# Branch A's attention output loaded and split inside branch B's chunks of a hybrid encoder layer, other slots for branch B's, branch weights by the sync queue

## The chip, the cores and the metric

The kernel runs on one core of a Trainium2 chip. The metric is the device time of one execution in microseconds; lower is better. The engines are named as in the profile: PE (TensorE matmul) with PEld (its weight loads), DVE (VectorE), ACT (ScalarE), POOL (GpSimd) and SP (SyncE, which here only issues DMAs). "us" is microseconds.

## The reference

One layer over 1024 tokens of width 1024, in fp32:

```
h = x + 1/2 * SwiGLU_1(RMSNorm(x))                       # d_ff 2816
u = RMSNorm(h)
[qA|kA|vA|qB|kB|vB|gA|gB] = u @ W_in                      # A: 8 heads; B: 8 heads, 2 kv heads; gates 1024 each
yA = NeighbourhoodAttention2D(qA, kA, vA) + relative bias
yB = WindowedGQA(rope(qB), rope(kB), vB), sink in the softmax
h = h + (sigmoid(gA) * (yA @ W_A) + sigmoid(gB) * (yB @ W_B)) @ W_out
h = h + 1/2 * SwiGLU_2(RMSNorm(h))
y = RMSNorm_final(h)
```

yA and yB are 512 wide, W_A and W_B are 512 x 1024, W_out is 1024 x 1024.

## The kernel before, in words

Every operand of a matmul is split into a high part (a cast to fp32r on ACT, line 95) and a low part (the rest, a subtraction on DVE, line 98). `split` does this. `mm3` (lines 146 to 153) then issues three matmuls for each product: high by high on line 149, high by low on 151, low by high on 153. Activations stand transposed, features on partitions.

The program's order in time: first FFN, the input projection, the attention, the branch matrices, the merge with W_out, the second FFN, the last norm. This case is about the stretch from the end of the attention to the start of the merge.

Storage is in fixed places. `ar[0]` to `ar[6]` are seven large tiles of four slots each; slot k is a 128x1024 piece of `ar[k // 4]`. During the attention `ar[0]`, `ar[6]`, `ar[1]` and `ar[4]` hold u, split. Three pools have few buffers: `raw` (4, for tiles just loaded), `xs` (2) and `ws` (8, split weights and the attention's transposed probabilities). A load can be issued only once its buffer is free.

The attention (lines 1434 to 1461) is a pipeline of 64 units, each with the steps `scores` (matmuls on lines 1377 and 1378, softmax on DVE and ACT), `turn` (transposes on line 1396, then a split) and `values` (matmuls on line 1410, whose `write` puts the result into `fa` or a DRAM tensor `y_d`). Between a unit's steps `filling` draws from the generator `fill`, which issues other matmuls so that PE has work:

- `gate(dc, steps)`: 8 steps of 6 matmuls, one 128-wide piece of the gate projection from u; `steps` says what is issued behind which step. Steps 0 to 3 read `ar[1]` and `ar[4]` (c = 4 to 7), steps 4 to 7 read `ar[0]` and `ar[6]`. The result is copied to an `xs` tile (line 1207) and stored to `g_d`.
- `branch_b`: eight chunks of 24 matmuls, yB @ W_B. Chunk dc needs its split weights (`fetch_w(dc)`, a load of a 128x1024 tile of `wab_d`, split during the first FFN), and yB, split, in the four pairs of slots `Y_B`. Each chunk ends with two operations on DVE that multiply by the gate (line 1280) into `merged(dc)`; the gate's tile is loaded by `fetch_gate` and opened by a tanh on ACT (`open_gate`).
- three quarters of the first two chunks of branch A.

`fetch_y` loads a 128x1024 tile of an attention output from `y_d` into a `raw` buffer, `split_y` splits it into a pair of slots. Branch B's slots are 4 to 7 (`ar[1]`) and 0 to 3 (`ar[0]`). Branch A's first three pairs are split at units 59, 60 and 62 of the attention; the fourth is written by the last attention units themselves.

Behind the attention the loop on line 1495 runs the chunks of branch A (i = 0 to 7), adds them into `merged` and forms combinations (`combine`). Then `down` (class `Down`, 28 entries of 12 matmuls) multiplies by W_out with Strassen's seven products. Each entry e needs two splits, its `prep`.

The order of instructions on each engine comes from the tile framework, which schedules by its own estimates; `pin` (lines 92 and 97) holds an instruction in program order on its engine. Each engine, and each of the two DMA-issuing queues (SP and POOL), works through its list in that order and waits where something isn't ready.

Of the kernel before, what the change touches and what calls it, by code (L numbers as in the profile page):

```python
# [36 lines left out]
def trunk_kernel(ctx, tc, x, xt, n1, wg1, wu1, wd1, nm, win, rpb, sink, wa, wb, wo,  # L37
# [39 lines left out]
    def slot(k):  # L77
        return ar[k // 4][:, k % 4, :]
# [15 lines left out]
    def split(dst_hi, dst_lo, src, eng=None, late=False):  # L94
        hi = nc.scalar.copy(dst_hi, src)  # L95
        if late:
            pin(hi)
        (eng or nc.vector).tensor_tensor(dst_lo, src, f32v(dst_hi), op=ALU.subtract)  # L98
# [415 lines left out]
    class Down:  # L514
# [2 lines left out]

        ORDER = ("P2", "P1", "P5", "P6", "P3", "P7", "P4")

        def __init__(self, n, w, scale, place, left=None, dram=None, loads={}, ring=(22, 24, 26), shift=0):  # L520
# [5 lines left out]
            self.TAIL = min(n, 5)  # L526
            self.ring, self.shift, self.RING = ring, shift, 4 + len(ring)
            self.W = self.Y = None

# [31 lines left out]
        def prep(self, e):  # L561
            k, p = self.seq[e]
            if k in self.dram:
                d = self.dk.index(k) * self.nd + p // 2
                self.load_left(d + 3)
                left = self.raw[d][:, p % 2, :]
            else:
                left = self.left(k, p)
            b11, b12, b21, b22 = [self.blocks(n, p)[:, 0, :] if n in self.loaded else None for n in ("B11", "B12", "B21", "B22")]
            eng = nc.gpsimd if self.n > self.RING else nc.vector  # L570
            if k == "P5":
                nc.vector.tensor_tensor(b11, b12, b11, op=ALU.subtract)
# [7 lines left out]
            split(s[:, :512], s[:, 512:], left)  # L580
            split(t[:, :512], t[:, 512:], dict(B11=b11, B12=b12, B21=b21, B22=b22)[SOURCE[k]])
            self.ent[e] = s, t

        def prep_until(self, n):
# [134 lines left out]
    wab_d = dram.tile([2 * NC8, P, 1024], F32R, name="wab_d")  # L719
    cast = {}  # L720

    def hs(dt):
# [11 lines left out]

    def wab_put(i):
        for k, a in enumerate(cast.pop(i)):
            nc.gpsimd.dma_start(wab_d[i, :, k * 512:k * 512 + 512], a)

    def behind_ffn1(n):
        down.at_end(n)  # L740
# [466 lines left out]
            nc.scalar.copy(gt[:, n * 512:(n + 1) * 512], bs[n])  # L1207
        nc.gpsimd.dma_start(g_d[dc * P:(dc + 1) * P, :], gt)

    Y_A, Y_B = ((12, 13), (14, 15), (20, 21), (22, 23)), ((4, 5), (6, 7), (0, 1), (2, 3))  # L1210

    def branch_mm(bs, w, y):

# [23 lines left out]
        a_mm.append((bs, branch_mm(bs, mix.pop(("w", NC8 + i)), Y_A)))  # L1237

    def merged(dc):
        return slot((16, 17, 18, 19, 24, 25, 26, 27)[dc])  # L1240

    def fetch_gate(dc):
        mix["rb", dc] = xs4() if dc % 2 else raw4()
        nc.sync.dma_start(mix["rb", dc], g_d[D + dc * P:D + (dc + 1) * P, :])

    def fetch_w(i):
        t = ws4()
        nc.gpsimd.dma_start(t, wab_d[i])
        mix["w", i] = [t[:, k:k + 512].rearrange("p (c f) -> p c f", f=P) for k in (0, 512)]

    def open_gate(dc):
# [2 lines left out]

    def branch_b():

        for g in (4, 6):
            new_ar(g, F32)
        split_y(Y_B[2], 2 * P, nc.vector)
        fetch_w(1)  # L1260
        for dc in range(NC8):
            bs = [bank("dg"[dc % 2]) for _ in range(2)]
            mm = branch_mm(bs, mix.pop(("w", dc)), Y_B)
            for c in range(4):
                drain(mm, 1)
                yield
                if c == 0:
                    if dc == 0:
                        split_y(Y_B[3], 3 * P, nc.vector)
                        open_gate(0)  # L1270
                    if dc + 1 < NC8:
                        fetch_gate(dc + 1)
                elif c == 1:
                    fetch_w(dc + 2)
                elif c == 3 and dc + 1 < NC8:
                    open_gate(dc + 1)
            rb = mix.pop(("rb", dc))
# [13 lines left out]
    def filler():  # L1291
        for dc, nxt in zip(gates, gates[1:] + [None]):
            if nxt is not None:
                yield from gate(dc, {4: lambda: mix.update(gate=load_w(win[0], GA + nxt * P))})
            else:
                yield from gate(dc, {0: lambda: [fetch_y(c * P) for c in range(2)],
                                     1: lambda: [fetch_w(0), fetch_gate(0)],
                                     4: lambda: [split_y(Y_B[0], 0, nc.vector), fetch_y(2 * P)],
                                     6: lambda: [split_y(Y_B[1], P, nc.vector), fetch_y(3 * P)]})
        yield from branch_b()  # L1300
        for i in range(2):
            branch_a(i)
# [131 lines left out]
    for n in range(1 << 30):  # L1434
# [13 lines left out]
            drain(prep, 1)  # L1448
        if n >= 26 and (n - 26) % 8 == 0 and n < 58:
            fetch_bias((n - 26) // 8)  # L1450
        if n in (56, 57, 59):
            fetch_y(512 + min(n - 56, 2) * P)
        if n in (59, 60, 62):
            split_y(Y_A[min(n - 59, 2)], 512 + min(n - 59, 2) * P, nc.vector)
        filling(n)
        if len(pipe) > 2 and pipe[2] is not None:
            values(pipe[2])
# [17 lines left out]
    def quarter(k, p):  # L1475
        m = merged(p + (4 if k in ("P2", "P4") else 0))
        return m[:, :512] if k in ("P1", "P2") else m[:, 512:]

    place = dict(B11=[(0, p) for p in range(4)], B21=[(0, 4 + p) for p in range(4)],
                 B12=[(1, p) for p in range(4)], B22=[(1, 4 + p) for p in range(4)])  # L1480
    loads = {t: [lambda d, t=t: load_h(t)] for t in range(NTT)}
    loads[0].append(lambda d: d.load_left(2))
    down = Down(4, wo[0], 0.5, place, quarter, {k: left_d[i] for i, k in enumerate(("P5", "P6", "P3", "P7"))},
                loads, (8, 10))

    def combine(p):
        a11, a12, a22 = [quarter(k, p) for k in ("P1", "P2", "P4")]
# [163 lines left out]
```

## Time and profile before

| | |
|---|---|
| time, median of 3 runs | 1932.38 us (1932.32 to 1932.75) |
| the profiled execution's own time | 1933.77 us |
| its span in the profile | 1932.0 us |
| PE busy | 1919.7 us (99%) |
| DVE busy | 1435.3 us (74%) |
| ACT busy | 940.3 us (49%) |
| POOL busy | 301.4 us (16%) |
| mean granted PE clock | 0.998 |

The profile's times run from the start of the span. A row of the timeline gives start, duration, engine, line, operation, output and input tile, and in brackets how long the engine had been idle and what ended that. A row that ends in "x2" joins two instructions; the duration of such a row, and of single matmuls, runs longer than the distance to the next row, since matmuls are pipelined. So the price of a matmul is the distance between starts.

### The profile page before, as it was taken

What the parts mean: (1) busy time and instruction counts of PE and PEld (TensorE: products, weight loads), DVE (VectorE), ACT (ScalarE), POOL (GpSimd) and SP (SyncE); (2) the same over time, 40 slices, a digit from 0 to 9 for tenths busy, and PEclk for the clock granted to TensorE, in tenths of its full rate; (3) what the DMA queues carried; (4) which work ended last, traced back from release to release, by engine and by line L of the source; (5) the groups of instructions that cost most, each with busy time, mean ns of one, the idle gap of its engine ahead of it and who ended that gap; (6) DMA issues with size and microseconds to landing.
All of it is one profiled execution on the core that took longest, in us unless ns stands there. A gap on an engine that the chain in (4) does not pass through costs nothing.

```text
span 1932.0 us, 25630 instructions
## 1 busy us (share of the span) xinstructions
PE 1919.7 (99%) x8956; PEld 1603.0 (83%) x8956; DVE 1435.3 (74%) x2511; ACT 940.3 (49%) x1826; POOL 301.4 (16%) x466
## 2 busy tenths in 40 slices
PE   9999999999999999999999999999999999999998
PEld 7888888888888888888888878888888888888886
DVE  8987766668966878677788846989676566569864
ACT  7532444444446543477788842365333333344453
POOL 0011111214400112211122011010111001005210
PEclk9999999999999999999999999999999999999999
DMA  6254556586454267854478386543422322492341
GB/s 267 94 173 166 176 177 193 172 294 246 124 171 150 108 200 239 257 163 99 115 174 202 135 297 234 180 153 120 147 96 102 130 86 106 143 354 103 114 143 61
DMA packets 163330, 321.78 MB, mean 167 GB/s; under 512 B 16256, under 2 KB 69888, under 8 KB 163200
## 3 DMA queue, kind: packets, MB, share of 16 engines
q1 hardware_dynamic: 127744, 216.82, 34.3%
q0 software_dynamic: 34736, 102.26, 16.4%
q8 instruction: 71, 1.16, 0.2%
q10 hardware_dynamic: 720, 1.05, 0.1%
q14 instruction: 59, 0.48, 0.1%
HBM read 222.04 MB, written 99.81 MB: 167 GB/s over the span
## 4 chain that ended last, share of the span: by engine, by line
PE 96%; DVE 2%; DMA 1%; ACT 1%; issue 0%; POOLq 0%; SPq 0%; POOL 0%; DVEq 0%
PE g L149 18%; PE g L151 18%; PE g L153 18%; PE d L153 12%; PE d L151 12%; PE d L149 12%; PE d L1396 2%; PE g L1415 1%; PE d L1377 1%; PE d L1378 1%; PE g L1410 1%; PE d L142 1%; DVE ar L98 0%; DMA raw<-y_d 0%; DMA raw<-in_w_in_dram 0%
## 5 line engine op out<-in xcount | busy, mean ns | idle before, releaser
L149 PE MATMUL g<-ar,ws 128*128 128x512 f32 x1128 | 423.2, 395 | 0.1
L153 PE MATMUL g<-ar,ws 128*128 128x512 f32 x1128 | 417.6, 390 | 0.0
L151 PE MATMUL g<-ar,ws 128*128 128x512 f32 x1128 | 417.6, 390 | 0.0
L149 PE MATMUL d<-ar,ws 128*128 128x512 f32 x736 | 282.3, 391 | 1.5 <-ACT ar L95 1.4
L151 PE MATMUL d<-ar,ws 128*128 128x512 f32 x736 | 282.0, 390 | 0.9 <-DVE ar L879 0.6
L153 PE MATMUL d<-ar,ws 128*128 128x512 f32 x736 | 281.8, 390 | 0.1
L153 PEld LDWEIGHTS g<-ar,ws 128*128 128x128 f32 x1128 | 212.0, 188 | 45.2
L151 PEld LDWEIGHTS g<-ar,ws 128*128 128x128 f32 x1128 | 212.0, 188 | 44.5
L149 PEld LDWEIGHTS g<-ar,ws 128*128 128x128 f32 x1128 | 206.6, 188 | 36.5 <-ACT xs L1207 0.6
L322 DVE TENSOR_TENSOR ws<-raw,ws 128x512 fp32r<-128x512 f32 x204 | 139.4, 689 | 83.4 <-ACT ws L319 82.5
L319 ACT CAST ws<-raw 128x512 fp32r<-128x512 f32 x204 | 125.2, 620 | 142.8 <-PE g L153 63.0
L149 PEld LDWEIGHTS d<-ar,ws 128*128 128x128 f32 x736 | 138.0, 188 | 31.0 <-ACT ar L95 1.8
L151 PEld LDWEIGHTS d<-ar,ws 128*128 128x128 f32 x736 | 138.1, 188 | 30.6 <-DVE ar L879 1.3
L153 PEld LDWEIGHTS d<-ar,ws 128*128 128x128 f32 x736 | 138.4, 188 | 29.7 <-DVE ws L322 0.8
L95 ACT CAST ws<-raw 128x512 fp32r<-128x512 f32 (+1 forms) x111 | 74.7, 673 | 137.0 <-PE d L153 62.9
L98 DVE TENSOR_TENSOR ws<-raw,ws 128x512 fp32r<-128x512 f32 (+1 forms) x111 | 89.1, 803 | 53.7 <-ACT ws L95 52.9
L426 POOL DMA_DIRECT2D hid<-fx x91 | 49.4, 543 | 373.1 <-DVE fx L486 247.4
L98 DVE TENSOR_TENSOR ws<-ar,ws 128x512 fp32r<-128x512 f32 x114 | 93.8, 828 | 11.5 <-ACT ws L95 11.5
L95 ACT CAST ar<-raw 128x512 fp32r<-128x512 f32 (+1 forms) x81 | 54.1, 670 | 88.5 <-PE g L151 54.4
L149 PE MATMUL g<-ws,ws 128*128 128x512 f32 x232 | 90.9, 392 | 0.0
L153 PE MATMUL g<-ws,ws 128*128 128x512 f32 x232 | 90.4, 390 | 0.0
L151 PE MATMUL g<-ws,ws 128*128 128x512 f32 x232 | 90.3, 389 | 0.0
(315 smaller groups left out, 3624.7 us busy)
## 6 DMA issues: line engine op xcount, KB each, us to landing
raw<-hid SPq DMA_DIRECT2D x70, 512.0 KB
hid<-fx POOLq DMA_DIRECT2D x91, 256.0 KB, 2.6
ar<-in_ffn_w_down_dram SPq DMA_DIRECT2D x32, 512.0 KB
raw<-in_ffn_w_up_dram SPq DMA_DIRECT2D x31, 512.0 KB
raw<-in_ffn_w_gate_dram SPq DMA_DIRECT2D x27, 512.0 KB
raw<-in_w_in_dram SPq DMA_DIRECT2D x27, 512.0 KB
hid<-fa POOLq DMA_DIRECT2D x51, 256.0 KB, 2.8
ar<-zs_d POOLq DMA_DIRECT2D x48, 256.0 KB, 6.4
```

Source lines behind the costliest of these rows:

```text
L95: hi = nc.scalar.copy(dst_hi, src)
L98: (eng or nc.vector).tensor_tensor(dst_lo, src, f32v(dst_hi), op=ALU.subtract)
L142: nc.tensor.transpose(pt[:, c * P:(c + 1) * P], xs[:, (half * 4 + c) * P:(half * 4 + c + 1) * P], ident)
L149: nc.tensor.matmul(b, lhs[0], r[0], start=first, stop=False, **kw)
L151: nc.tensor.matmul(b, lhs[0], r[1], start=False, stop=False, **kw)
L153: nc.tensor.matmul(b, lhs[1], r[0], start=False, stop=last, **kw)
L319: nc.scalar.copy(w[0][:, :512], a)
L322: nc.vector.tensor_tensor(w[0][:, 512:], a, f32v(w[0][:, :512]), op=ALU.subtract)
L426: nc.gpsimd.dma_start(hid[PRODUCTS.index(p), i], src)
L1377: nc.tensor.matmul(b[:, :nw], un["q"][s], un["kd"][s][:, k0 * P:k1 * P], start=True, stop=False)
L1378: nc.tensor.matmul(b[:, :nw], un["q"][s], un["kl"][s][:, k0 * P:k1 * P], start=False, stop=True)
L1396: nc.tensor.transpose(pt[:, i * P:(i + 1) * P], un["pr"][s][:, i * P:(i + 1) * P], ident)
```

## The change

- **Branch B's slots**: 4 to 7 and 16 to 19 (`ar[1]` and `ar[4]`) in place of 4 to 7 and 0 to 3. The first four of `merged` go to 0 to 3 in place of 16 to 19, and in the merge W_out's blocks B11 and B21 go to `ar[4]` in place of `ar[0]`.
- **Branch B's splits**: all four are issued behind steps 3 to 6 of the last gate; before, two of them stood behind steps 4 and 6, and two in `branch_b`.
- **Branch A's three loads and splits** move from the attention's units 56 to 62 into branch B's chunks (loads in chunks 0 to 2, splits in chunks 2 to 4).
- **Weights**: `fetch_w` issues on SP; before, on POOL. `wab_d` is declared fp32 for that, with the same bytes.
- **Gate tiles** of branch B all use `xs` buffers; before, every second one used `raw`.
- **Merge**: its casts in `prep` are pinned (`late=True`).

```diff
-    Y_A, Y_B = ((12, 13), (14, 15), (20, 21), (22, 23)), ((4, 5), (6, 7), (0, 1), (2, 3))
+    Y_A, Y_B = ((12, 13), (14, 15), (20, 21), (22, 23)), ((4, 5), (6, 7), (16, 17), (18, 19))
...
-        return slot((16, 17, 18, 19, 24, 25, 26, 27)[dc])
+        return slot((0, 1, 2, 3, 24, 25, 26, 27)[dc])
...
-        mix["rb", dc] = xs4() if dc % 2 else raw4()
+        mix["rb", dc] = xs4()
...
-        nc.gpsimd.dma_start(t, wab_d[i])
+        nc.sync.dma_start(f32v(t), wab_d[i])
...
-        for g in (4, 6):
+        for g in (0, 6):
             new_ar(g, F32)
-        split_y(Y_B[2], 2 * P, nc.vector)
...
                     if dc == 0:
-                        split_y(Y_B[3], 3 * P, nc.vector)
                         open_gate(0)
...
+                elif c == 2 and dc < 5:
+                    if dc < 3:
+                        fetch_y(512 + dc * P)
+                    if dc >= 2:
+                        split_y(Y_A[dc - 2], 512 + (dc - 2) * P, nc.vector)
...
                 yield from gate(dc, {0: lambda: [fetch_y(c * P) for c in range(2)],
-                                     1: lambda: [fetch_w(0), fetch_gate(0)],
-                                     4: lambda: [split_y(Y_B[0], 0, nc.vector), fetch_y(2 * P)],
-                                     6: lambda: [split_y(Y_B[1], P, nc.vector), fetch_y(3 * P)]})
+                                     1: lambda: fetch_w(0),
+                                     2: lambda: fetch_y(2 * P),
+                                     3: lambda: split_y(Y_B[0], 0, nc.vector),
+                                     4: lambda: [split_y(Y_B[1], P, nc.vector), fetch_y(3 * P)],
+                                     5: lambda: [split_y(Y_B[2], 2 * P, nc.vector), fetch_gate(0)],
+                                     6: lambda: split_y(Y_B[3], 3 * P, nc.vector)})
...
-        if n in (56, 57, 59):
-            fetch_y(512 + min(n - 56, 2) * P)
-        if n in (59, 60, 62):
-            split_y(Y_A[min(n - 59, 2)], 512 + min(n - 59, 2) * P, nc.vector)
...
-    place = dict(B11=[(0, p) for p in range(4)], B21=[(0, 4 + p) for p in range(4)],
+    place = dict(B11=[(4, p) for p in range(4)], B21=[(4, 4 + p) for p in range(4)],
...
-                loads, (8, 10))
+                loads, (8, 10), late=True)
```

How this moves instructions is seen in the engines' lists. PE keeps its 8950 matmuls and transposes, and their order differs only around the last gate and the first chunk of branch B.

ACT's list at the end of the attention, before. Casts into `ar_494` and `ar_493` are the high parts of yB (`ar[1]` and `ar[0]`), L1207 copies the last gate's result, L1346 belongs to the attention:

```order
L95 CAST ar_494_4625<-raw_1484_10133 128x8x8x16
L1346 COPY s1_747_6722<-g_1508_10255 64x256
L95 CAST ar_494_4625<-raw_1485_10135 128x8x8x16
L1207 COPY xs_1511_10293<-g_1476_10096 128x512
L1207 COPY xs_1511_10293<-g_1477_10097 128x512
L1346 COPY s1_747_6722<-g_1510_10282 64x256
L95 CAST ar_493_4624<-raw_1507_10247 128x8x8x16
L95 CAST ar_73_563<-fa_73 128x512
L95 CAST ar_493_4624<-raw_1509_10274 128x8x8x16
L1253 ACTIVATE raw_1491_10161<-raw_1491_10161 128x1024
```

The same place in the change's list, where `ar_541` is `ar[4]`, L1352 is the attention's copy, and the casts of `ws` belong to its last `turn`:

```order
L95 CAST ar_494_4625<-raw_1481_10123 128x8x8x16
L1352 COPY s1_747_6722<-g_1499_10212 64x256
L95 CAST ws_1500_10223<-d_1502_10225 128x2x128
L95 CAST ws_1501_10224<-d_1503_10230 128x2x128
L95 CAST ar_494_4625<-raw_1482_10125 128x8x8x16
L1352 COPY s1_747_6722<-g_1505_10245 64x256
L95 CAST ar_541_5004<-raw_1494_10182 128x8x8x16
L95 CAST ar_541_5004<-raw_1504_10237 128x8x8x16
L1207 COPY xs_1508_10285<-g_1473_10086 128x512
L1207 COPY xs_1508_10285<-g_1474_10087 128x512
```

All four casts now stand ahead of the copies of the last gate; before, the third and the fourth stood behind them.

POOL's list before, with the first weights (L1248) behind the last stores of branch A's output (L1355) and of the gates (L1208):

```order
L1355 DMA y_d_3438<-fa_73 128x512
L1208 DMA g_d_3436<-xs_1475_10092 128x1024
L1248 DMA ws_1490_10159<-wab_d_86 128x1024
L1248 DMA ws_1514_10301<-wab_d_86 128x1024
L1248 DMA ws_1518_10322<-wab_d_86 128x1024
```

SP's list in the change, from the second half of branch B's y on (L1221 loads y, L1244 a gate tile, L1472 is the residual h):

```order
L1221 DMA raw_1494_10182<-y_d_3438 128x1024
L1472 DMA fx_1558_10623<-h_d_3431 128x1024
L1472 DMA fx_1559_10624<-h_d_3431 128x1024
L1221 DMA raw_1504_10237<-y_d_3438 128x1024
L1244 DMA xs_1506_10258<-g_d_3436 128x1024
L1248 DMA ws_1487_10147<-wab_d_86 128x1024
L1248 DMA ws_1511_10291<-wab_d_86 128x1024
L1221 DMA raw_1516_10318<-y_d_3438 128x1024
L1248 DMA ws_1515_10310<-wab_d_86 128x1024
L1248 DMA ws_1520_10345<-wab_d_86 128x1024
L1221 DMA raw_1521_10353<-y_d_3438 128x1024
L1248 DMA ws_1525_10380<-wab_d_86 128x1024
```

The sixteen weight loads now stand in one list with the loads of y, of the gates and of W_out, and branch A's y (`raw_1516_10318` is its first tile) stands behind branch B's first two weight tiles.

ACT's list in the merge, before: L1289 opens branch A's gate tiles, the casts are those of `prep` (`ar_1578` are entries 4 and 5, `ws` the others):

```order
L1289 ACTIVATE raw_1563_10643<-raw_1563_10643 128x1024
L95 CAST ar_1578_10778<-ar_1561_10628 128x512 x2
L95 CAST ar_1578_10778<-ar_1512_10297 128x512
L95 CAST ws_1583_10848<-ar_1513_10298 128x512
L95 CAST ws_1584_10849<-ar_1561_10628 128x512
L1289 ACTIVATE raw_1565_10665<-raw_1565_10665 128x1024
L1289 ACTIVATE raw_1568_10699<-raw_1568_10699 128x1024
L95 CAST ar_1578_10778<-ar_1512_10297 128x512
L1289 ACTIVATE raw_1571_10739<-raw_1571_10739 128x1024
```

The same in the change (L1292 opens the gate tiles):

```order
L1292 ACTIVATE raw_1563_10643<-raw_1563_10643 128x1024
L1292 ACTIVATE raw_1565_10665<-raw_1565_10665 128x1024
L1292 ACTIVATE raw_1568_10699<-raw_1568_10699 128x1024
L1292 ACTIVATE raw_1571_10739<-raw_1571_10739 128x1024
L1292 ACTIVATE raw_1575_10774<-raw_1575_10774 128x1024
L95 CAST ws_1583_10848<-ar_1510_10290 128x512
L95 CAST ws_1584_10849<-ar_1561_10628 128x512
L95 CAST ws_1585_10854<-ar_1510_10290 128x512
```

Every cast of `prep` now stands behind the last opening of a gate tile, and so do DVE's subtractions that go with them: four splits and four subtractions of W_out's blocks that DVE had among branch A's chunks come later.

More of the change, by code (lines that the diff above doesn't have):

```diff
@@ L518, in trunk_kernel, with __init__ @@
         ORDER = ("P2", "P1", "P5", "P6", "P3", "P7", "P4")
-        def __init__(self, n, w, scale, place, left=None, dram=None, loads={}, ring=(22, 24, 26), shift=0):
+        def __init__(self, n, w, scale, place, left=None, dram=None, loads={}, ring=(22, 24, 26), shift=0, late=False):
             self.n, self.w, self.scale, self.place, self.left, self.dram, self.loads = n, w, scale, place, left, dram, loads
@@ L525, in __init__ @@
             self.raw, self.nraw, self.done, self.ent, self.tiles, self.loaded = {}, 0, 0, {}, {}, {}
-            self.TAIL = min(n, 5)
+            self.TAIL, self.late = min(n, 5), late
             self.ring, self.shift, self.RING = ring, shift, 4 + len(ring)
@@ L579, in prep @@
             s, t = (ws4(), ws4()) if i < 4 else pair_slots(self.ring[i - 4])
-            split(s[:, :512], s[:, 512:], left)
-            split(t[:, :512], t[:, 512:], dict(B11=b11, B12=b12, B21=b21, B22=b22)[SOURCE[k]])
+            split(s[:, :512], s[:, 512:], left, None, self.late)
+            split(t[:, :512], t[:, 512:], dict(B11=b11, B12=b12, B21=b21, B22=b22)[SOURCE[k]], None, self.late)
             self.ent[e] = s, t
@@ L718, in trunk_kernel @@
     a_order = [dc for p in range(4) for dc in (p, p + 4)]
-    wab_d = dram.tile([2 * NC8, P, 1024], F32R, name="wab_d")
+    wab_d = dram.tile([2 * NC8, P, 1024], F32, name="wab_d")
     cast = {}
@@ L736, in wab_put @@
         for k, a in enumerate(cast.pop(i)):
-            nc.gpsimd.dma_start(wab_d[i, :, k * 512:k * 512 + 512], a)
+            nc.gpsimd.dma_start(wab_d[i, :, k * 512:k * 512 + 512], f32v(a))
     def behind_ffn1(n):
```

## The prediction

> **What bounds the kernel now.** First the page's busy times, then PE's own waits around the branches.
>
> ```profile
> PE 1919.7 (99%) x8956; PEld 1603.0 (83%) x8956; DVE 1435.3 (74%) x2511; ACT 940.3 (49%) x1826; POOL 301.4 (16%) x466
> ```
>
> PE is the bound: of a span of 1932.0 us only 12.3 are without a matmul, and the change leaves all matmuls in. It can gain or lose only where PE stands still or runs slowly. PE's waits between 1100 and 1140 us (sum, times, longest):
>
> ```profile
> PE d L149 <- ACT ar L95: 1.4, 1, 1.4
> PE d L1396 <- DVE fa L1387: 0.9, 1, 0.9
> PE d L151 <- DVE ar L98: 0.3, 1, 0.3
> ```
>
> Three waits, 2.6 in sum, all at what the change moves. ACT's timeline and the chain that ended last show why:
>
> ```profile
> 1099.09 1.05 ACT L95 CAST ws<-raw 128x1024 fp32r<-128x1024 f32 x1 [2.22 <-DMA raw<-in_w_in_dram]
> ```
>
> ```profile
> 1119.81 6.14 DMA raw<-y_d
> 1125.97 1.05 ACT ar L95
> 1127.05 1.24 DVE ar L98
> ```
>
> The 0.9: ACT stands 2.22 until the last gate's weights land, and softmax work is queued behind that cast. The 1.4 and 0.3: branch B's fourth yB tile lands at 1125.97 and is then cast (1.05) and subtracted (1.24) while PE already needs it. PE's timeline gives the prices:
>
> ```profile
> 1098.18 0.81 PE L1396 MATMUL d<-ident,fa 128*128 128x128 f32 x6
> 1098.76 0.70 PE L149 MATMUL g<-ar,ws 128*128 128x512 f32 x2
> ...
> 1100.22 0.87 PE L1410 MATMUL g<-ws,fx 128*128 128x256 f32 x6
> 1100.93 0.34 PE L1377 MATMUL d<-ar,ar 128*128 128x384 f32 x1
> ...
> 1101.63 0.40 PE L149 MATMUL g<-ar,ws 128*128 128x512 f32 x1
> ...
> 1121.12 0.63 PE L149 MATMUL d<-ar,ws 128*128 128x512 f32 x2
> ...
> 1136.16 0.61 PE L149 MATMUL d<-ar,ws 128*128 128x512 f32 x2
> ...
> 1141.61 0.61 PE L149 MATMUL g<-ar,ws 128*128 128x512 f32 x2
> ```
>
> From start to start, six transposes take 0.58, six matmuls of `values` 0.71, four of `scores` 0.70, and a chunk of 24 large matmuls 5.45 (1136.16 to 1141.61), so 0.227 each.
>
> **The last gate.** From 1100.93 to the first chunk of branch B at 1121.12 PE has 48 gate matmuls (10.90), three `scores` (two of 0.70, one with two thirds of the columns, 0.47), 22 transposes (three sixes 1.74, four 0.39) and 28 `values` matmuls (3.31): 18.2 of the 20.2 that pass. 2.0 are lost, the 0.89 among them and the rest beside it, where matmuls were slotted in singly. The change takes branch A's splits (ACT and DVE) out of this stretch, and the gate's weights stand in SP's list ahead of all loads of y, so that they land early. What is left is ACT's softmax chain at the first `turn`: between nothing and the 0.9 of now. I take 0.4, since the copy of the gate before still stands ahead of the softmax scale on ACT. Gain: **1.6**.
>
> **The first two chunks.** They should take 48 times 0.227, 10.9; they take 15.04 (1121.12 to 1136.16): 4.1 lost. 1.7 are the waits. Another part is the clock:
>
> ```profile
> 1125.00:1130.00 5.00, 3.30 (x10) 2.04 (x9) 1.28 (x3) 2.95 (x3) 0.26 (x1) 0.85 1.00 367
> 1130.00:1135.00 5.00, 5.00 (x19) 4.02 (x18) 1.24 (x2) 1.06 (x1) 0.53 (x1) 0.81 1.12 415
> 1135.00:1140.00 5.00, 5.00 (x23) 4.13 (x22) 1.28 (x2) 2.01 (x2) 0.53 (x1) 1.00 1.06 406
> ```
>
> Each row is a window: its length, then busy time and count of PE, PEld, DVE, ACT and POOL, then the granted clock, the DMA share and GB/s. The clock's shortfall is 0.15 x 5 + 0.19 x 5 = 1.7, right behind the waits, and gone from 1135 on. I count it as a consequence of the wait. The remaining 0.7 are matmuls issued in another order behind the wait.
>
> By the Trainium skill, "TensorE: Matmul & The Clock Gate", Part 1, the clock falls to half behind an idle window of about 3.4 us. The trace has a low clock behind an idle time of 1.41 and 0.29, so the trace is stricter than the page. By the page so short a wait would not be the cause, and the 1.7 would stay.
>
> Will the wait go? Branch B's slots are all in `ar[1]` and `ar[4]`, free behind step 3 of the last gate, so all four splits can run behind steps 3 to 6. The y tiles need only `raw` buffers that are free before 1100. The prices of the tail:
>
> ```profile
> 1113.79 0.86 ACT L95 CAST ws<-d 128x384 fp32r<-128x384 f32 x2
> 1114.54 0.52 ACT L1383 ACTIVATE fa<-fa,nmx 128x256 f32<-128x256 f32 x1
> 1115.82 0.51 ACT L1388 ACTIVATE fa<-fa,rc 128x256 f32<-128x256 f32 x1
> 1116.13 0.41 DVE L1347 TENSOR_TENSOR s<-g,s 64x256 f32<-64x256 f32 x1
> 1116.58 0.58 DVE L1350 TENSOR_TENSOR fa<-g,s 64x128 f32<-64x128 f32 x2
> 1117.34 0.76 DVE L98 TENSOR_TENSOR ws<-d,ws 128x256 fp32r<-128x256 f32 x2 [0.18 <-ACT ws L95]
> ```
>
> Count from the end of step 3. ACT first has half of the last unit's softmax and its casts (0.7 + 0.9 + 0.5 = 2.1), then the first yB cast: out at 3.2; DVE's part at 4.4. DVE then has three more splits (3 x 1.24 = 3.7) and the last units' pieces (two of 0.41 and 0.58, and 0.76: 2.7): the fourth split is done at 10.8. PE meanwhile has four steps (5.4), ten transposes (1.0) and sixteen `values` matmuls (1.9), 8.3, and then three quarters of chunk 0 (4.1) and two matmuls until it reads the fourth tile's low part: 12.9. Slack 2. Nothing takes the wait's place, and the clock stays up. Gain: **4.1**.
>
> **Weights by SP.** Sixteen loads leave POOL. The first two were released so:
>
> ```profile
> 1107.72 0.55 POOL L1248 DMA_DIRECT2D ws<-wab_d  x1 [0.37 <-PE g L1410]
> 1115.81 0.54 POOL L1248 DMA_DIRECT2D ws<-wab_d  x1 [7.53 <-PE g L1410]
> ```
>
> Both wait for a `ws` buffer from the attention, as they will on SP. There the first stands behind y tiles and a gate tile that are released long before it. At 6.1 to land (the y tile of the chain, under full DMA load) the first is there at 1114, the second at 1122; they are needed at 1119.5 and 1125. The others each have a chunk of 5.45 or more to spare: SP blocks on a gate tile until the chunk two before is evicted, and weights for three later chunks stand ahead of that. PSUM lets PE run ahead of a late eviction by four chunks' banks. Branch A's splits (1.05 and 1.24, three times) lie in chunks in which ACT and DVE are mostly free, 30 us ahead of their use. I take 0; ends: nothing, or one wait as large as the 1.4 of now.
>
> **The merge.** Pinned `prep` puts eight DVE operations of 0.6 (4.9) behind branch A's last openings. Rows of the place:
>
> ```profile
> 1180.00:1260.00 80.00, 80.00 (x355) 66.24 (x354) 75.85 (x119) 29.29 (x48) 8.69 (x16) 1.00 0.51 180
> ...
> 1199.59 1.06 ACT L1289 ACTIVATE raw<-raw 128x1024 f32<-128x1024 f32 x1 [2.23 <-DMA raw<-g_d]
> ...
> 1212.33 0.39 PE L149 MATMUL d<-ws,ws 128*128 128x512 f32 x1
> ...
> 1217.14 0.68 DVE L98 TENSOR_TENSOR ws<-ar,ws 128x512 fp32r<-128x512 f32 x1
> ```
>
> DVE is busy 75.85 of 80 there (fourth number), so order matters. `down` starts at 1212.33 and an entry takes 2.73. Entry 3's last split is done at 1217.8, entry 3 starts at 1220.5: 2.7 spare, unchanged, since the evictions of branch A's last chunk set it. Entries 4 and 5, split early before, now come next, four operations of 0.61 and one of `combine`: done 7.2 and 8.5 behind the start, needed 10.9 and 13.6 behind it. So 3.7 spare. Later entries lose at most the 4.9, and DVE's list was some 10 ahead of PE. Cost: **0**.
>
> **Sum.** 1.6 + 4.1 = 5.7. The profiled execution's 1933.77 (1932.0 of span and 1.8 around it) would become 1928.1. Its time is 1.4 above the median of 1932.38; against the median the forecast is **1926.7**.
>
> **Rivals.** *The low clock stays*: the gap goes, but some short wait, or a cause other than the gap, still brings the shortfall of 1.7. For it speaks that the gap was only 1.7 itself; against it that the shortfall begins behind the gap and nowhere else in the branches. Time: 1926.7 + 1.7 = 1928.4. Chance 0.08.
>
> *The splits come late*: the four yB splits share ACT and DVE with the attention's last units. If two splits' worth (2 x 2.3) lies ahead of them beyond my count, PE waits 4.6 - 2.0 = 2.6, and the low clock costs 1.7 again: 1931.0. For it speaks that ACT and DVE are nearly full in the attention; against it the count. Chance 0.08.
>
> *Slower, by a late gate tile in the merge*: `prep`'s casts are pinned behind the opening of the last gate tile (1199.59 now), and DVE's first `prep` subtraction stands ahead of the evictions of branch A's last three chunks. If that tile lands late by x, ACT, DVE and then PE stop. DVE has about 2 free until 1212 and entry 3 has 2.7, so PE waits x - 5, and it is slower than before from x = 11. Opening has waited 9.46 for such a tile:
>
> ```profile
> 1168.96 1.06 ACT L1289 ACTIVATE raw<-raw 128x1024 f32<-128x1024 f32 x1 [9.46 <-DMA raw<-g_d]
> ```
>
> SP's list is longer now, with weights and W_out's blocks among the gate tiles. With x = 17, PE would wait 12: 1926.7 + 12 = 1938.7. Against it: its load waits for the same buffer as now, and all weights are issued ahead of it by then. Chance 0.05.
>
> By the Trainium skill, "DMA: Bandwidth & Descriptors", Queues, rings and completion order, each DMA engine takes turns between the queues it has work for; one queue then serves weights strictly behind the y tiles. That makes this rival's lateness possible, and no run here shows it yet.
>
> **Numbers.** The forecast has 0.79. Its own range is 1926.0 (the whole 6.1 recovered, and 0.3 of scatter) to 1927.9 (the 0.9 wait stays, and a wait of 0.7 in the chunks). To hold 8 in 10 I take in the low clock and part of a small new wait: 1925.9 to 1929.2. A measurement of this kernel can tell about 0.2% from no change, 3.9 us, so "same" is 1928.5 to 1936.2. The forecast and half of the first rival lie below (0.82), the late splits, the other half and a part of the forecast's tail within (0.13), the slower one above (0.05).
>
> **What would show it.** Right: no wait of PE above 0.5 between 1100 and 1135, clock 1.00 throughout, the first chunk of branch B near 1119.5 and the third 10.9 behind it, and no wait of PE between 1170 and 1240. Wrong: a wait of `g` or `d` on L149 for `ws` (weights late), on L151 for L98 (splits late), on DVE's L98 of `ws` at the start of `down` (the merge), or a window of low granted clock without a gap ahead of it.

## The result and the profile after

The changed kernel takes 1928.22 us (median of 13 runs, 1927.66 to 1929.63) against 1932.1 (13 runs, 1930.91 to 1933.53): 3.9 us less, ratio 0.998 with an interval of 0.9971 to 0.9989. The profiled execution took 1928.8, its span is 1927.0, 5.0 less than the profiled one of before. The two differences, 3.9 and 5.0, are not the same thing, and most of the experiments below are about that.

The page's busy times and PE's waits in the whole run (sum, times, longest):

```profile
PE 1917.4 (100%) x8956; PEld 1602.4 (83%) x8956; DVE 1437.9 (75%) x2511; ACT 942.2 (49%) x1826; POOL 293.1 (15%) x450
```

```profile
PE g L798 <- POOL ident masks.py:199: 1.5, 1, 1.5
PE d L151 <- DVE ar L879: 0.6, 2, 0.3
```

Neither wait is near the change: at 1100 to 1140 and at 1170 to 1240 there is none. PE's timeline from the last gate on, and the windows that had the low clock before (length, busy and count of PE, PEld, DVE, ACT, POOL, then clock, DMA share, GB/s):

```profile
1101.61 0.34 PE L1383 MATMUL d<-ar,ar 128*128 128x384 f32 x1
...
1102.31 0.82 PE L1402 MATMUL d<-ident,fa 128*128 128x128 f32 x6
...
1120.26 0.63 PE L149 MATMUL d<-ar,ws 128*128 128x512 f32 x2
...
1124.82 0.61 PE L151 MATMUL d<-ar,ws 128*128 128x512 f32 x2
...
1131.17 0.62 PE L149 MATMUL d<-ar,ws 128*128 128x512 f32 x2
```

```profile
1125.00:1130.00 5.00, 5.00 (x23) 4.14 (x23) 1.28 (x2) 0.00 (x0) 0.00 (x0) 1.00 0.60 215
1130.00:1135.00 5.00, 5.00 (x23) 4.13 (x22) 1.28 (x2) 2.21 (x3) 0.00 (x0) 1.00 1.03 410
```

From the scores to chunk 0 it is 1101.61 to 1120.26, 18.65 (before 20.19); the transposes of the first `turn` (1102.31) follow the scores without a stop. What differs ahead of it is the last gate's weights. Their load, issued at 1093.71 before (first row), is now issued 59 us earlier, at 1034.28 (the second of the two that the second row joins), and ACT's cast of them begins at 1096.09 without a wait, where before it stood 2.22 and began at 1099.09. Branch A's splits, which left this stretch too, were not tried apart from that:

```profile
1093.71 5.36 DMA raw<-in_w_in_dram
```

```profile
1033.80 1.01 SPq L104 DMA_DIRECT2D raw<-in_w_in_dram  x2
```

```profile
1096.09 1.06 ACT L95 CAST ws<-raw 128x1024 fp32r<-128x1024 f32 x1
```

From chunk 0 to the third chunk it is 10.91 (before 15.04), with PE busy throughout and the clock at 1.00. SP's, ACT's and DVE's rows show why:

```profile
1098.43 0.32 SPq L1221 DMA_DIRECT2D raw<-y_d  x1
```

```profile
1117.51 2.00 ACT L95 CAST ar<-raw 128x1024 fp32r<-128x1024 f32 x2
```

```profile
1120.61 1.23 DVE L98 TENSOR_TENSOR ar<-raw,ar 128x1024 fp32r<-128x1024 f32 x1
```

Branch B's fourth yB tile is issued at 1098.43, 21 us earlier than the 1119.81 of before, and its split ends at 1121.84, 3.0 ahead of the matmuls that read its low part (1124.82). The load goes out as DVE's split of the last gate's weights ends (1098.41), so it seems to take their `raw` buffer. Before, the tile itself landed at 1125.97. The merge, as a window, as the first matmul of `down`, and as DVE's four pinned subtractions for entries 4 and 5:

```profile
1180.00:1260.00 80.00, 80.00 (x355) 66.26 (x354) 73.48 (x115) 32.03 (x54) 8.02 (x15) 1.00 0.51 174
```

```profile
1207.33 0.39 PE L149 MATMUL d<-ws,ws 128*128 128x512 f32 x1
```

```profile
1213.01 2.49 DVE L98 TENSOR_TENSOR ar<-ar,ar 128x512 fp32r<-128x512 f32 x4
```

They end 8.2 behind the start of `down`, ahead of the 10.9 at which entry 4 begins.

Laid side by side matmul by matmul, the profiles of before and after differ in one other place: in the first FFN, at 517 and 520, where the changed kernel's run lost 0.6. The change does not touch that place, and the second profile of the unchanged kernel (below) lost 0.7 there too. From 1133 to the end the distance stays constant. So the profiled gain is 0.6 more than the spans say, 5.6: 1.5 from the last gate and 4.1 from the first two chunks.

### The profile page after: what moved, and what is told of

Its sections match the earlier page's. It is cut to its first block, busy times and chain, and to the rows that moved or that the text cites. A ratio compares the mean times of both kernels' runs of the same rounds, so it can differ in the third digit from the quotient of the medians.

```text
span 1927.0 us, 25619 instructions
## 1 busy us (share of the span) xinstructions
PE 1917.4 (100%) x8956; PEld 1602.4 (83%) x8956; DVE 1437.9 (75%) x2511; ACT 942.2 (49%) x1826; POOL 293.1 (15%) x450
## 4 chain that ended last, share of the span: by engine, by line
PE 97%; DVE 2%; DMA 0%; issue 0%; ACT 0%; SPq 0%; POOLq 0%; POOL 0%; DVEq 0%
PE g L149 18%; PE g L151 18%; PE g L153 18%; PE d L153 12%; PE d L149 12%; PE d L151 12%; PE d L1402 2%; PE g L1421 1%; PE g L1416 1%; PE d L1383 1%; PE d L1384 1%; PE d L142 1%; DVE ar L98 0%; DMA fx<-in_xt_dram 0%; DMA u_d<-s 0%
## 5 line engine op out<-in xcount | busy, mean ns | idle before, releaser
L1389 ACT ACTIVATE fa<-fa,nmx 128x385 f32<-128x385 f32 (+3 forms) x128 | 75.7, 592 | 32.0 <-DVE nmx L1386 29.0
L149 PE MATMUL g<-ws,ws 128*128 128x512 f32 x232 | 90.9, 392 | 0.0
L153 PE MATMUL g<-ws,ws 128*128 128x512 f32 x232 | 90.4, 390 | 0.0
```

What stands on the lines that cost most here:

```text
L149: nc.tensor.matmul(b, lhs[0], r[0], start=first, stop=False, **kw)
L153: nc.tensor.matmul(b, lhs[1], r[0], start=False, stop=last, **kw)
L1389: nc.scalar.activation(pr, pr, AF.Exp, scale=-1.0, bias=nmx[:, s:s + 1], accum_out=ssum[:, s:s + 1])
```

## Experiments

Times are medians; "before" is the kernel before on the same chip in the same session (1932.1 to 1932.3 each time).

| kernel | us | against before | ratio, interval |
|---|---|---|---|
| A moved alone | 1931.9 | -0.2 | 0.9997 (0.9988 to 1.0006) |
| B's slots alone | 1929.87 | -2.3 | 0.9989 (0.9980 to 0.9998) |
| weights by SP alone | 1931.93 | -0.2 | 0.9995 (0.9986 to 1.0004) |
| merge pinned alone | 1931.43 | -0.7 | 0.9996 (0.9987 to 1.0005) |
| A moved and B's slots | 1928.45 | -3.8 | 0.9980 (0.9971 to 0.9989) |
| changed, weights by POOL | 1928.34 | -3.9 | 0.9980 (0.9971 to 0.9989) |
| changed, merge unpinned | 1928.24 | -4.0 | 0.9979 (0.9971 to 0.9988) |

### The parts one by one

**Branch A moved alone.**

```diff
-        if n in (56, 57, 59):
-            fetch_y(512 + min(n - 56, 2) * P)
-        if n in (59, 60, 62):
-            split_y(Y_A[min(n - 59, 2)], 512 + min(n - 59, 2) * P, nc.vector)
...
+                elif c == 2 and dc < 5:
+                    if dc < 3:
+                        fetch_y(512 + dc * P)
+                    if dc >= 2:
+                        split_y(Y_A[dc - 2], 512 + (dc - 2) * P, nc.vector)
```

> The kernel before with one part of the change: branch A's three loads and splits go into branch B's chunks (loads in chunks 0 to 2, splits in 2 to 4). Branch B keeps its old slots and its old places of splits, weights stay on POOL, the merge unpinned. Theory 'slots' (the prediction's: the wait in the first chunk stands because branch B's third and fourth yB splits must wait for the last gate to free their slots): the 0.89 of wait at the last gate goes (about 1.5 gained with what lies beside it), the wait in chunk 0 stays, at 1.7: median about 1.5 below the kernel before. Rival 'raw buffers' (the fourth yB tile landed at 1125.97 because branch A's tiles held the buffers; the slots are free at about 1119.7, and two casts of 1.05 with a subtraction of 1.24 behind each would make chunk 0's reads at 1123.0 and 1124.3): both waits go, 3.6 to 4.0 below the kernel before, as much as the whole change. On the clock: theory 'grid' (both low spells of the profile of before lie on one grid of 3.41 us that runs free of the program, so a gap of 1.7 brings a low spell only where it falls into one window): where a wait of 1.4 to 1.7 remains, some executions have the low spell and most have not. Rival 'behind the gap': every execution with that wait has a low spell of 3.4 us and loses 1.7 by it.

Measured: 1931.9, not told from no change, with 11 executions from 1929.82 to 1934.71. On the clock it went as "grid" has it: four of the eleven read a mean clock of 0.998, the other seven 0.999. The profiled execution is one of the shortest. PE's scores and chunk 0, and its waits:

```profile
1101.55 0.34 PE L1382 MATMUL d<-ar,ar 128*128 128x384 f32 x1
...
1120.17 0.63 PE L149 MATMUL d<-ar,ws 128*128 128x512 f32 x2
```

```profile
PE d L151 <- DVE ar L98: 0.5, 1, 0.5
```

The last gate takes 18.62: this part alone removes the whole 1.5 there. But chunk 0 still waits, and mostly longer than in this profile, so that the median shows nothing of it. Neither theory had that. The repeats below tell why.

**Branch B's slots alone** (with its splits behind steps 3 to 6 of the last gate; the places of `merged` and of W_out's blocks move as in the change and are not shown again).

```diff
...
-    ... ((4, 5), (6, 7), (0, 1), (2, 3))
+    ... ((4, 5), (6, 7), (16, 17), (18, 19))
...
-                                     4: lambda: [split_y(Y_B[0], 0, nc.vector), fetch_y(2 * P)],
-                                     6: lambda: [split_y(Y_B[1], P, nc.vector), fetch_y(3 * P)]})
+                                     2: lambda: fetch_y(2 * P),
+                                     3: lambda: split_y(Y_B[0], 0, nc.vector),
+                                     4: lambda: [split_y(Y_B[1], P, nc.vector), fetch_y(3 * P)],
+                                     5: lambda: [split_y(Y_B[2], 2 * P, nc.vector), fetch_gate(0)],
+                                     6: lambda: split_y(Y_B[3], 3 * P, nc.vector)})
```

> The kernel before with another part alone: branch B's y in the change's slots (4 to 7 and 16 to 19), its four splits behind steps 3 to 6 of the last gate; branch A's loads and splits stay in the attention, weights on POOL, merge unpinned. Theory 'slots': the wait of 1.7 in chunk 0 goes, the 0.89 at the last gate stays: 2.0 to 2.5 below the kernel before by the medians. Rival 'raw buffers': seven y tiles now pass through four raw buffers within the last units, branch B's third and fourth land as late as before or later, and the new splits, pinned ahead of the last gate's copies on ACT, hold those up: a wait of 1 to 5 at the last gate or in chunk 0, no gain or up to 4 slower.

Measured: 2.3 below before, as the theory "slots" had it. PE's only wait between 1090 and 1240, and the starts of chunks 0 and 2:

```profile
PE d L1397 <- DVE fa L1388: 0.6, 1, 0.6
```

```profile
1121.34 0.63 PE L149 MATMUL d<-ar,ws 128*128 128x512 f32 x2
...
1132.25 0.62 PE L149 MATMUL d<-ar,ws 128*128 128x512 f32 x2
```

The two chunks take 10.91, as in the changed kernel; the wait at the last gate stays (0.6 here, 0.89 in the first profile). Seven y tiles in four buffers held up no matmul. Branch B's fourth tile is issued 6 us earlier than the 1119.81 of before:

```profile
1113.83 0.32 SPq L1221 DMA_DIRECT2D raw<-y_d  x1
```

**Weights by SP alone**, and **the merge pinned alone**.

```diff
...
-        nc.gpsimd.dma_start(t, wab_d[i])
+        nc.sync.dma_start(f32v(t), wab_d[i])
...
```

> The kernel before with a third part alone: fetch_w issues on SP, wab_d declared fp32 with the same bytes. The prediction put 0 on it within the whole change. Alone, SP's list has the first weights ahead of branch B's third y tile and the second and third weights ahead of its fourth. Theory 'free': PE order and the 1.7 of wait as before, within 0.5 of the kernel before. Rival 'queue': the fourth y tile waits on SP behind weights whose ws buffers come free later, it lands later than 1126 by 1 to 4 us, the wait in chunk 0 grows by that, and 1 to 4 slower. On the clock: with a wait of 3.4 or more both theories give a low spell; with 1.7, 'grid' gives it in some executions only.

```diff
-                loads, (8, 10))
+                loads, (8, 10), late=True)
```

> The kernel before with the fourth part alone: the casts of prep in the merge pinned behind branch A's openings. Everything up to 1150 us is the kernel before, with its waits of 0.89, 1.41 and 0.29. The prediction put 0 on the pinning. Theory 'cost 0': within 0.3 of the kernel before, no wait of PE from 1170 to 1240. Rival 'late gate tile': a wait of PE on DVE's L98 at the start of down, 1 to 10 slower. On the clock: 'grid' gives this profile a low spell near 1128 with a chance of about one in four, and a span 1.7 shorter than the 1932.0 of the profile of before where there is none; 'behind the gap' gives it always.

Measured: -0.2 and -0.7, both within their intervals. The pinned kernel's profile has the waits of before (1.1 at the last gate, 1.0 and 0.3 in chunk 0), a span of 1929.7 and no low clock there. A single profile cannot bear on the expected chance of one in four; the count of executions further down (4 of 69) says that it was too high. With weights by SP, the first profile has no wait in chunk 0 at all, but the 11 executions go from 1929.74 to 1934.18, so that one profile does not stand for them; "queue" is not borne out as a steady cost either. Whether the pinning alone brings some tenths stays open.

**The two parts undone in the changed kernel.** The edits are the two above, backwards.

> The changed kernel with the weights issued by POOL again. Prediction's step: weights by SP cost and bring nothing, so 3.9 below the kernel before, as the changed kernel, within 0.4. Rival 'shared transfers' (in the four runs so far a y tile that is issued on SP at about 1119 takes 6.14, 5.73 and 5.61 to land while POOL's queue is moving weights, and 3.78 with weights and y in one list): branch B's fourth y tile and branch A's tiles land later and unevenly; the fourth yB split, spare by about 3 in the changed kernel, is still in time, but gate tiles and branch A's tiles, 7 to 14 us to land behind POOL's weights, hold up ACT's list: 1 to 3 slower than the changed kernel, and executions scatter over 2 to 5 us.

> The changed kernel without the pinning of prep's casts in the merge. Prediction's step: the pinning costs 0, so 3.9 below the kernel before within 0.3, no wait of PE from 1170 to 1240. Rival 'pinning gains' (the kernel before with the pinning alone came out 0.7 below it, interval from -2.5 to +1.0): 0.4 to 1.0 slower than the changed kernel.

Measured: 1928.34 and 1928.24, the changed kernel's time both times, with 11 executions each within 1.8 us. The 1 to 3 us and the scatter of "shared transfers" are not there, and "pinning gains" shows nothing (0.02): the prediction's two zeros hold, though a few tenths either way could not be told here.

**The two parts that are left, together**: branch A moved and branch B's slots (and gate tiles in `xs`), weights on POOL, merge unpinned.

> The kernel before with the two parts that touch the waits together: branch A's loads and splits in branch B's chunks, branch B's new slots and early splits (and gate tiles in xs buffers, as in the change). Weights stay on POOL, the merge unpinned. Theory 'two parts': these make the whole gain, 3.9 below the kernel before, within 0.4, executions within 2 us of each other. Rival 'all needed': weights by SP or the pinning give part of it, and this stays 0.5 or more short.

Measured: 1928.45, 3.8 below before, so these make the gain; by the medians the first two alone bring 0.2 and 2.3. The gate tiles in `xs` came only together with the others, so their share is not shown. In the profiles of this kernel, of the changed one and of the two with a part undone, the last gate takes 18.65 or 18.66 and the first two chunks 10.91. The executions, 1927.44 to 1930.27, scatter more than the 2 us that were expected. From 1090 to 1240 PE has one wait left in this profile, at the start of `down`, on the gated sum of branch A's last chunk:

```profile
1209.83 0.50 PE L149 MATMUL d<-ws,ws 128*128 128x512 f32 x1 [0.64 <-DVE raw L1517]
```

The same wait is 0.2 in the three profiles of branch A moved alone, all unpinned as well, and absent from the changed kernel and from its unpinned form. A pinned `prep` may spare it in some executions; at a few tenths no median here can tell.

### The low clock

**The kernel before, once more.**

> The kernel before, unchanged, for a second profile of it. Theory 'grid': its spans of 33 executions have a median of 1930.35 and only two show a clock of 0.998, as the profiled 1932.0 did, so most executions have the waits of the first chunk and no low spell: a span of 1930.0 to 1930.8, waits of about 1.4 and 0.3 in chunk 0, clock 1.00 from 1100 to 1140, and from the chunk's start to the third chunk's 13.3 where the first profile had 15.04. Rival 'behind the gap': the low spell is there again, span near 1932.

PE's waits from 1090 to 1240, the scores, chunk 0 and chunk 2 in its timeline, and the landing in the chain of waits:

```profile
PE d L149 <- ACT ar L95: 0.9, 1, 0.9
PE d L1396 <- DVE fa L1387: 0.8, 1, 0.8
PE d L151 <- DVE ar L98: 0.3, 1, 0.3
```

```profile
1101.98 0.34 PE L1377 MATMUL d<-ar,ar 128*128 128x384 f32 x1
...
1122.06 0.63 PE L149 MATMUL d<-ar,ws 128*128 128x512 f32 x2
...
1135.07 0.61 PE L149 MATMUL d<-ar,ws 128*128 128x512 f32 x2
```

```profile
1120.76 5.67 DMA raw<-y_d
```

The waits are there, the last gate takes 20.08, the two chunks take 13.01, and no low clock shows. The span of 1931.3 is 0.5 above what was expected, for other reasons: matmul by matmul against the first profile, 0.7 was lost at the place in the first FFN, 0.4 at the start of `down`, and 0.4 in small pieces elsewhere. "Behind the gap" is already in trouble, though this gap is shorter (0.9 and 0.3) than the first profile's (1.4 and 0.3).

**Stops of PE put into the second FFN.**

```diff
+    def pe_gap(k):
+        b = bank("g")
+        pin(nc.tensor.transpose(b[:, :P], ident, ident))
+        pin(nc.scalar.copy(gap_t, b[:, :64]))
+        for _ in range(k):
+            pin(nc.gpsimd.tensor_copy(gap_t, gap_t))
+        b = bank("g")
+        pin(nc.tensor.transpose(b[:64, :P], gap_t, ident))
...
-    drain(hg[2])
+    GAPS = [0, 2, 4, 6, 8, 11] * 4
+    for n, _ in enumerate(hg[2]):
+        if n >= 24 and n % 24 == 0 and GAPS:
+            pe_gap(GAPS.pop(0))
```

> The changed kernel with 23 stops of PE put into the second FFN, about 16 us of matmuls apart: a transpose of the identity, a copy of its result on ACT, then 0, 2, 4, 6, 8 or 11 small copies on POOL, and a second transpose that reads the last copy. PE can't go on before. Nothing else is changed, results included. Theory 'grid': each low spell starts and ends at a multiple of 3.41 us from every other, and it follows only a window of that grid in which PE stood for more than some share, about half; stops of 1 to 2.5 us then bring a spell in some cases and not in others, those of 3 and more nearly always. Rival 'behind the gap': a spell begins a fixed time behind each stop longer than about 1.4, whatever the place. Price of a spell by both: 3.41 at half speed, 1.7.

PE's wait at the stops, and four windows, of 3.41 each:

```profile
PE g L1545 <- POOL gap_t L1543: 24.6, 18, 2.4
```

```profile
1539.00:1542.42 3.42, 1.42 (x7) 0.84 (x5) 0.80 (x2) 0.74 (x2) 2.81 (x11) 1.00 0.20 77
1542.42:1545.83 3.41, 3.13 (x8) 2.53 (x9) 0.00 (x0) 0.00 (x0) 0.22 (x1) 0.50 0.00 0
...
1433.19:1436.60 3.41, 1.55 (x8) 1.29 (x9) 0.78 (x2) 0.00 (x0) 1.56 (x5) 1.00 0.00 0
1436.60:1440.01 3.41, 3.41 (x17) 2.82 (x16) 1.20 (x2) 1.56 (x3) 0.00 (x0) 1.00 0.00 0
```

In 18 of the 23 stops PE waited for POOL, up to 2.4 us; none reached the 3 us from which a spell was expected nearly always. Only two brought a low spell, at 1542.42 and 1614.10, each 3.41 long at 0.50. They lie 71.68 apart, 21 times 3.413; counted from the first rise of the clock in the same trace (6.42) they begin at 450 and 471 times 3.413. In the first profile of before, the spell at 1128.51 begins 329 times 3.413 behind the first rise (5.52). So in these traces the clock is set anew on a grid of 3.413 us, and what PE did in the window that just ended fits as what sets it. For each window I counted the time between a matmul's start and the next beyond its price (the busy numbers above count a matmul's modelled tail, so they read a little high). The two windows ahead of the spells had 2.16 and 2.14 us of standing; the next longest, 1433.19 in the rows, had 1.95 and no spell behind it. The length of a stop does not decide: the longest, 2.8 us in all at 1648, was cut by the grid into 1.3 and 1.5 and brought no spell, while one of 2.3 at 1610, with 2.14 in one window, did. The expectation "about half" was too low: by these counts the bound lies between 57% and 63% of a window. In the first profile of before the window is this:

```profile
1125.09:1128.51 3.42, 1.72 (x7) 0.80 (x6) 1.23 (x1) 2.54 (x3) 0.17 (x1) 1.00 0.98 350
1128.51:1131.92 3.41, 3.41 (x9) 2.64 (x10) 1.28 (x2) 1.47 (x2) 0.53 (x1) 0.50 1.08 410
```

Its standing, counted alike, is 1.59 + 0.11 + 0.45 = 2.15: just over the bound, and all of it in one window.

**Branch A moved alone, twice more.**

> The first experiment's kernel again (branch A moved alone), for another profile: its 11 spans went from 1928.0 to 1932.9, and the profiled one was among the shortest. Theory 'landing': the last gate is 1.5 shorter each time, and what varies is when branch B's fourth yB tile lands (1123.56 in the first profile, wait 0.53 in chunk 0); each us that it lands later is a us of wait in chunk 0, and over about 2.1 us of standing in one window of the clock's grid add 1.7. Rival 'elsewhere': the wait of chunk 0 stays near 0.5, and the time goes in later chunks or at the start of down.

> The same kernel and the same theories once more, since one profile shows one landing only. Over the three profiles, 'landing' has span minus (landing of the fourth yB tile) constant within 0.5, the spell of 1.7 apart; 'elsewhere' has not.

The second profile: the yB load in the chain (issue, time to landing), PE's waits, and its grid's windows:

```profile
1118.13 7.46 DMA raw<-y_d
```

```profile
PE d L149 <- ACT ar L95: 1.8, 1, 1.8
PE d L151 <- DVE ar L98: 0.5, 1, 0.5
```

```profile
1124.66:1128.07 3.41, 1.07 (x5) 0.40 (x3) 1.39 (x2) 2.46 (x3) 0.00 (x0) 1.00 1.01 310
1128.07:1131.48 3.41, 3.41 (x9) 2.63 (x10) 1.73 (x3) 1.12 (x2) 0.53 (x1) 0.50 1.06 416
```

The third: ACT's cast that waited for the tile, the waits, the windows:

```profile
1125.62 1.04 ACT L95 CAST ar<-raw 128x1024 fp32r<-128x1024 f32 x1 [3.25 <-DMA raw<-y_d]
```

```profile
PE d L149 <- ACT ar L95: 1.7, 1, 1.7
PE d L151 <- DVE ar L98: 0.5, 1, 0.5
```

```profile
1122.43:1125.85 3.42, 2.56 (x11) 1.48 (x9) 1.28 (x2) 0.23 (x1) 1.05 (x2) 1.00 1.09 350
1125.85:1129.26 3.41, 2.01 (x8) 1.36 (x9) 2.04 (x3) 2.60 (x4) 0.00 (x0) 1.00 1.00 351
1129.26:1132.67 3.41, 3.41 (x17) 2.82 (x16) 1.07 (x2) 0.76 (x1) 0.53 (x1) 1.00 1.07 412
```

This pair settles it. The tile lands at 1125.6 in both, PE waits 1.8 and 0.5 in the one, 1.7 and 0.5 in the other. In the second profile the whole gap falls into one window (2.78 of standing), and the next runs at 0.50; in the third the grid's line at 1125.85 cuts the gap (1.28 and 1.79), and the clock stays at 1.00. The last gate takes 18.66 and 18.64, the two chunks 15.67 and 14.01, and the spans are 1932.4 and 1930.8: 1.6 apart, with the phase of the grid as the only difference that the traces show there.

The same three profiles bear out "landing": span minus landing is 1928.7 - 1123.6 = 805.1, 1930.8 - 1125.6 = 805.2, and 1932.4 - 1125.6 - 1.7 of spell = 805.1.

**Weights by SP alone, once more.**

> The third experiment's kernel again (weights by SP alone), whose spans went from 1928.0 to 1932.4. In its first profile the fourth yB tile landed at 1123.54, 3.78 behind its issue, and chunk 0 had no wait. Theory 'landing': here it lands later, up to 1127, and chunk 0 waits by as much; the wait of 0.9 at the last gate is the same. Rival 'elsewhere': chunk 0 has no wait, and the time goes to a weight tile or a gate tile in later chunks.

The chain's load and PE's wait in chunk 0, and behind them ACT's cast of the same tile in this kernel's first profile:

```profile
1119.68 5.91 DMA raw<-y_d
```

```profile
PE d L149 <- ACT ar L95: 1.2, 1, 1.2
```

```profile
1123.64 1.04 ACT L95 CAST ar<-raw 128x1024 fp32r<-128x1024 f32 x1
```

"Landing" again: issued at nearly the same time, the tile lands at 1125.6 here, while in the first profile the cast began at 1123.64 with no wait for it. Chunk 0 waits 1.2, less than the 2.0 that the tile is late, and the span is 1.6 longer. So SP's list does not by itself make the landing early; a load that is issued at 1118 to 1120, among the weights, lands in time or 2 us late.

## Why the prediction came out as it did

**What held.** PE was the bound, and all of the gain lies between 1095 and 1135. The last gate gave 20.19 - 18.65 = 1.54, forecast 1.6, though by two errors that cancel: the stretch's floor is 18.65 and not 18.2 (singles and short groups take longer than their prices in groups), and of the 0.4 that was left for ACT's softmax chain nothing came. The first two chunks went from 15.04 to 10.91, the forecast 4.1 to the tenth, with the splits in time (spare 3.0, forecast 2). Its reading of the 4.1 was off in one part that cost it nothing: the 0.7 put down to "matmuls issued in another order" is standing of PE as well. Counted between starts, PE stood 2.4 us in these two chunks, 0.7 more than the listed waits, and in the second profile of before the 2.1 that are lost are standing in full. Weights by SP and the pinned merge cost nothing that the medians show (0.1 and 0.0 when each is undone). Of the rivals, the splits were not late, and no gate tile held up `prep`.

**What failed** is one step of the sum: "Its time is 1.4 above the median of 1932.38; against the median the forecast is 1926.7." It takes a gain that was worked out from one execution off the median of others. That execution was longer than the median because it held the low spell, and the spell was 1.7 of the gain. Most executions of the kernel before have no spell: of 69 that came with these experiments, the mean clock reads 0.998, as in the first profile, in 4. That is a lower bound, since the clock is rounded: the second profile of A moved alone reads 0.999 with its spell. But the 69 spans have a median of 1930.4, 1.6 below the first profile's 1932.0, which is about the spell's price. What the change takes from such an execution is the 1.5 of the last gate (20.08 to 18.65 against the second profile of before) and 2.1 in the chunks (13.01 to 10.91), 3.6; by the first profile without its spell, 1.5 + 4.1 - 1.7 = 3.9. The medians say 3.9. The term was not wrong in kind but priced for the wrong population: the forecast of 1926.7 should have been 1928.4. The rival "the low clock stays" has the same time, because it leaves the same 1.7 out of the gain, but for a reason that the trace refutes: in the changed kernel no low clock is left there at all. So there is luck in the forecast. The measured 1928.22 lies above the forecast's own range (1926.0 to 1927.9), and it falls into the stated range (1925.9 to 1929.2) because that was widened for this rival and a small new wait, neither of which came.

The prediction saw that the spell stands behind the gap, and took it for a fixed consequence. By the Trainium skill, "TensorE: Matmul & The Clock Gate", Part 1, the window is 3413 ns long and free-running, so that it does not start anew with the kernel. The traces agree to the third digit (3.413, whole multiples of it). That section of the Trainium skill draws from it that a kernel's warm-up depends on where in the window its first matmul falls. The profiles here show the same of a stop in mid-kernel, which the section does not say: a term from a spell belongs into a forecast of the median only with its frequency. The same section of the Trainium skill puts half clock behind an idle window; here 2.14 us of standing out of 3.41 were enough and 1.95 were not, so the measurement is stricter.

**What it did not see**: how much the two parts need each other. Branch A moved alone frees the last gate (18.6 in all three profiles) and leaves branch B's fourth load where it was, among the weights. Its landing scatters by 2 us, and the later one, 1125.6, is hardly earlier than the 1125.97 of before, so that most of the 1.5 turns into a longer wait in chunk 0 (1.7 and 0.5 where it was 1.4 and 0.3). The medians alone could not show this, with intervals of 1.7 us to either side; the profiles do. With the load at 1098.43 there is nothing left to scatter: the changed kernel's executions lie within 2.0 us, those of A moved alone within 4.9.

## What to carry to other kernels

Before a term from a profile is taken off a median, ask whether the profiled execution is a typical one: compare its time and its mean clock with those of the other runs. In these runs a short stop of PE costs its length always, and 1.7 more only where some 2.1 us of standing fall into one window of the clock's grid; count that part with its frequency. Parts that each remove one wait of a chain should be priced together, and a load that decides a wait is worth more early and far from other transfers than its mean landing time suggests.

## What the hardware showed that was not expected

- The granted clock changed only on a grid of 3.413 us that has its own phase in each profiled execution. A low spell at 0.50 lasted one window exactly (3.41) and cost 1.6 to 1.7 us.
- It followed windows with 2.14, 2.15, 2.16 and 2.78 us of standing, and no window with 1.95 or less. In the run with stops, eighteen waits of PE, up to 2.4 us long, brought only two spells.
- The same y tile, issued within 0.3 us of the same time, landed 5.6 us later in one execution and 7.4 to 7.5 in the next two (A moved alone: 1123.6 and 1125.6, issued at 1118.0 to 1118.2).
